# A 3x3 convolution on one core: input pairs loaded two at a time, two output pairs stored by one transfer each, and one image's store cut in halves

## The chip, the core and the metric

The kernel runs on one core of a Trainium2 chip. The metric is the device time of one execution in microseconds (us). Before the change it is 127.98 us, the median of three runs (127.71 to 128.12). One further execution was profiled; that profile is what is read here.

The engines that appear: PE multiplies matrices, DVE and POOL do elementwise work, ACT copies and converts, SP and ACT issue DMA transfers. A transfer is split over 16 DMA engines. What SP issues runs on queue q1 of each of them, what ACT issues on queue q10, so each DMA engine has one queue from SP and one from ACT.

## The reference

```python
batch, c_in, h, w, c_out = 16, 64, 64, 64, 128      # float32
x_pad = np.pad(x, ((0, 0), (0, 0), (1, 1), (1, 1)), mode='constant')
for b, co, ci, kh, kw:
    output[b, co] += weight[co, ci, kh, kw] * x_pad[b, ci, kh:kh+h, kw:kw+w]
```

The input is 16 images of 64 channels (16.8 MB), the output 16 images of 128 channels (33.6 MB). All of it passes through the DMA engines once.

## The kernel before

**Tiling.** Two images of 64 channels fill the 128 partitions, so the batch is eight pairs, p = 0 to 7 in the code. A pair's input is one tile `raw` of 128 partitions with 16 KB each, 2 MB in all. Its output is two tiles `ot` (one for each image, 128 output channels, 16 KB in each partition), again 2 MB each. Output rows are made two at a time, with a transform over the rows (Winograd's): for each block of 8 row pairs PE makes three groups of sums in PSUM, U (line 180), A (190) and Bt (193). ACT copies U to `ut` (184), and DVE adds `ut` to A for the even rows (192) and to Bt for the odd rows (195) and writes `ot`. A pair has four such blocks.

**Getting a pair ready.** Before PE can start on a pair, POOL must have made the row sums `ss` (line 70; for pair p+1 it is called at the start of pair p), and ACT must have converted the rows to 16 bits, `xs` (line 103; a quarter in each block of the pair before, right behind the block's two copies of U). ACT works in program order: a conversion that waits for its input holds up the copies of U behind it.

**Where things lie.** There are ten places of 16 KB in each partition, `home0` to `home9`, shared by inputs and outputs. `raw_home` and `out_home` (44, 45) say which place a pair's input and its two images take. A place is written anew only when its former content has been used or stored: a wait on a conversion, a sum, or the landing of a transfer.

**Transfers.** SP issues the weights, then the inputs of pairs 0 to 5 at the start (52 to 54). After block 3 of each pair SP stores the pair's first image (197), and after the first two pairs it loads pair 6 and pair 7 (200, 201). The second image goes onto a list (199) and is stored by ACT in the next pair, behind the copies of U (186, 187; for pair 0 not before block 2 of pair 1). The last pair's two images are stored in halves, after block 1 and after block 3 (`halves`, 123, 124). SP, too, works in order: a load that waits for its place holds up the stores behind it. So the order of work around the change is the order written in the program, engine by engine.

Of the kernel before, what the change touches and what calls it, by code (L numbers as in the profile page):

```python
# [8 lines left out]
F32 = mybir.dt.float32  # L9
# [4 lines left out]
def kernel(  # L14
# [6 lines left out]
    nc = tc.nc  # L21
    B, CI, H, W = x.shape
    CO = weight.shape[0]
    assert H == 64 and W == 64 and CI == 64 and CO == 128 and B % 2 == 0
    NP = B // 2
    RB = 8

    keep = tc.keep_in_program_order
    x_rows = x.rearrange("b c h w -> (b c) h w")
    out_rows = out.rearrange("b co h w -> b co h w")  # L30
# [5 lines left out]
    opool = ctx.enter_context(tc.tile_pool(name="opool", bufs=1))  # L36
# [4 lines left out]
    nc.sync.dma_start(w_raw, w_flat)  # L41


    raw_home = [0, 1, 2, 3, 4, 5, 0, 6]
    out_home = [(6, 7), (8, 9), (1, 2), (7, 3), (8, 4), (9, 5), (1, 2), (7, 3)]
    raws = {}

    def load(p):
        raws[p] = opool.tile([128, H, W], F32, tag=f"home{raw_home[p]}", name="raw")
        keep(nc.sync.dma_start(raws[p], x_rows[128 * p : 128 * p + 128, :, :]))  # L50

    AHEAD = 6
    for p in range(AHEAD):
        load(p)
    x0 = raws[0]
    ident = const.tile([128, 128], F16)
    make_identity(nc, ident)
# [7 lines left out]
    def sums(eng, p, src, lo, n):  # L65
        if p not in ss:
            ss[p] = spool.tile([128, H // 2, W], F16, tag="ss", name="ss")
        v = src.rearrange("p (j i) c -> p j i c", i=2)
        keep(
            eng.tensor_add(  # L70
                ss[p][:, lo : lo + n, :], v[:, lo : lo + n, 0, :], v[:, lo : lo + n, 1, :]
            )
        )
# [26 lines left out]
    def cast(copy, p, lo, hi):  # L100
        if p not in xs:
            xs[p] = xpool.tile([128, H, W], F16, tag="xs", name="xs")
        keep(copy(xs[p][:, lo:hi, :], raws[p][:, lo:hi, :]))  # L103
# [17 lines left out]

    whole = {3: (0, 64)}
    halves = {1: (0, 32), 3: (32, 64)}
    cuts_of = [(whole, whole)] * (NP - 1) + [(halves, halves)]

    def store(eng, p, b2, ot, lo, hi):
        return eng.dma_start(
            out_rows[2 * p + b2, :, lo:hi, :],
            ot.rearrange("p j i c -> p (j i) c")[:, lo:hi, :],
        )  # L130

    for p in range(NP):
        if p + 1 < NP:
            for lo in (0, 16):
                sums(nc.gpsimd, p + 1, raws[p + 1], lo, 16)
        ots = [
            opool.tile([128, H // 2, 2, W], F32, tag=f"home{k}", name="ot")
            for k in out_home[p]
        ]
        for blk in range(4):  # L140
            j0 = blk * RB

            def group(wi_rows):

                tiles = [
                    psum.tile([128, RB, W], F32, tag="acc", name="acc") for _ in range(2)
                ]
                n = 3 * len(wi_rows)
                i = 0
                for wi, off in wi_rows:  # L150
                    for kw in (1, 0, 2):
                        c_lo, c_hi = max(0, 1 - kw), min(W, W + 1 - kw)
                        for b2 in range(2):
                            p0 = 64 * b2
                            lo, hi = j0, j0 + RB
                            if off is None:
                                rhs = ss[p][p0 : p0 + 64, lo:hi, c_lo + kw - 1 : c_hi + kw - 1]
                            else:
                                while 2 * lo + off < 0:
                                    lo += 1  # L160
                                while 2 * (hi - 1) + off > H - 1:
                                    hi -= 1
                                first = 2 * lo + off
                                last = 2 * (hi - 1) + off
                                rhs = xs[p][
                                    p0 : p0 + 64,
                                    first : last + 1 : 2,
                                    c_lo + kw - 1 : c_hi + kw - 1,
                                ]
                            nc.tensor.matmul(  # L170
                                tiles[b2][:, lo - j0 : hi - j0, c_lo:c_hi],
                                Wt[p0 : p0 + 64, wi, kw, :],
                                rhs,
                                start=i == 0,
                                stop=i == n - 1,
                            )
                        i += 1
                return tiles

            U = group([(G1, None)])  # L180
            us = []
            for b2 in range(2):
                ut = upool.tile([128, RB, W], F32, tag="ut", name="ut")
                keep(nc.scalar.copy(ut, U[b2]))  # L184
                us.append(ut)
            while held and (p, blk) not in ((1, 0), (1, 1)):
                keep(store(nc.scalar, *held.pop(0)))
            for piece in later.get((p, blk), ()):
                cast(nc.scalar.copy, *piece)
            A = group([(G21, 1), (G0, -1)])  # L190
            for b2 in range(2):
                nc.vector.tensor_add(ots[b2][:, j0 : j0 + RB, 0, :], A[b2], us[b2])  # L192
            Bt = group([(G01, 0), (G2, 2)])
            for b2 in range(2):
                nc.vector.tensor_add(ots[b2][:, j0 : j0 + RB, 1, :], Bt[b2], us[b2])  # L195
            if blk in cuts_of[p][0]:
                keep(store(nc.sync, p, 0, ots[0], *cuts_of[p][0][blk]))
            if blk in cuts_of[p][1]:
                held.append((p, 1, ots[1], *cuts_of[p][1][blk]))
            if blk == 3 and p + AHEAD < NP:  # L200
                load(p + AHEAD)
    while held:
        keep(store(nc.scalar, *held.pop(0)))

# [29 lines left out]
```

## Time and profile before

| what | value |
|---|---|
| median of three runs | 127.98 us |
| the profiled execution, device time | 128.16 us |
| its span, from the first to the last event shown | 126.4 us |
| PE busy | 107.9 us, 85% of the span |
| DVE busy | 84.2 us, 67% |
| ACT busy | 65.8 us, 52% |
| POOL busy | 37.2 us, 29% |
| bytes moved by DMA | 50.77 MB, mean 402 GB/s |
| transfers on q1 / q10 | 18 / 9 |
| clock that PE was granted | 0.963 in the mean; full speed until the last matmul |

How to read it: a busy share is a mean over the whole span. The bytes moved, divided by the span, are a rate; whether it is near what the DMA engines can do is seen from how busy they are in each stretch of the span, and from how long one packet takes.

### The profile page before, as it was taken

The numbers are of one execution on the slowest core, as the hardware profiler recorded it, in microseconds if no ns is written. First come the engines' busy times: TensorE is split into PE (matmuls) and PEld (weight loads), VectorE is DVE, ScalarE is ACT, GpSimd is POOL, SyncE is SP. The second block draws the span as 40 slices with busy tenths as digits, with TensorE's granted clock in tenths as the row PEclk, the third lists the DMA queues.
The fourth block names the chain that finished last, engine by engine and source line by source line (L and its number), as shares of the span: only waits on it lengthen the run. The fifth ranks groups of instructions, "written<-read, shape, count | busy, mean of one in ns | idle before, by whom it ended". The sixth has DMA issues, their size and how long they took to land.

```text
span 126.4 us, 2450 instructions
## 1 busy us (share of the span) xinstructions
PE 107.9 (85%) x984; PEld 53.1 (42%) x984; DVE 84.2 (67%) x135; ACT 65.8 (52%) x98; POOL 37.2 (29%) x23
## 2 busy tenths in 40 slices
PE   0689999999999999999999999999999999970000
PEld 0534444444444444444444555555555555530000
DVE  1029987877777778777729977777877787771000
ACT  4128569966666657666664666666666633320000
POOL 2227685900590049004900193009400000000000
PEclk9999999999999999999999999999999999999555
DMA  5899999999899999999999999999999999999960
GB/s 161 363 441 446 425 420 420 430 451 394 332 430 430 438 425 420 428 430 441 425 410 430 425 446 430 415 425 425 436 441 415 425 410 420 449 392 420 438 254 10
DMA packets 3898, 50.77 MB, mean 402 GB/s; under 512 B 432, under 2 KB 432, under 8 KB 560
## 3 DMA queue, kind: packets, MB, share of 16 engines
q1 hardware_dynamic: 2592, 33.85, 64.1%
q10 hardware_dynamic: 1296, 16.78, 31.2%
q8 instruction: 7, 0.11, 0.3%
q14 instruction: 3, 0.02, 0.0%
HBM read 17.07 MB, written 33.55 MB: 401 GB/s over the span
## 4 chain that ended last, share of the span: by engine, by line
PE 79%; DMA 6%; DVE 2%; issue 1%; DVEq 0%; ACT 0%; SPq 0%; ACTq 0%
PE acc L170 79%; DMA raw<-in_x_dram 6%; DVE ot L192 1%; DVE ss L70 1%; DVE ot L195 0%; DVEq L229 0%; ACT ut L184 0%; SPq L41 0%; DVEq L192 0%; ACTq L184 0%
## 5 line engine op out<-in xcount | busy, mean ns | idle before, releaser
L170 PE MATMUL acc<-xs,Wt 64*128 64x504 f16 (+3 forms) x768 | 90.3, 373 | 0.2 <-DVE ot L192 0.2
L170 PEld LDWEIGHTS <-Wt 64*128 64x128 f16 x960 | 50.4, 94 | 53.9 <-issue 1.9
L192 DVE TENSOR_TENSOR ot<-acc,ut 128x512 f32<-128x512 f32 x64 | 41.1, 684 | 21.6 <-PE acc L170 16.2
L184 ACT COPY ut<-acc 128x512 f32<-128x512 f32 x64 | 34.4, 589 | 38.1 <-issue 21.5
L70 POOL TENSOR_TENSOR ss<-raw 128x1024 f16<-128x1024 f32 x14 | 32.8, 2364 | 45.1 <-issue 33.2
L195 DVE TENSOR_TENSOR ot<-acc,ut 128x512 f32<-128x512 f32 x64 | 41.0, 683 | 0.0
L103 ACT CAST xs<-raw 128x1024 f16<-128x1024 f32 (+1 forms) x30 | 31.6, 1060 | 3.4 <-DMA raw<-in_x_dram 3.3
L170 PE MATMUL acc<-ss,Wt 64*128 64x504 f16 (+1 forms) x192 | 28.7, 377 | 0.6 <-DVE ss L70 0.6
L70 DVE TENSOR_TENSOR ss<-raw 128x512 f16<-128x512 f32 x4 | 3.3, 866 | 7.5 <-DMA raw<-in_x_dram 7.5
L88 PE MATMUL wp<-ident,w 128*64 128x128 f16 x18 | 1.3, 328 | 4.3 <-POOL w L59 4.3
L103 POOL CAST xs<-raw 128x1024 f16<-128x1024 f32 (+1 forms) x2 | 3.0, 1518 | 4.6 <-DMA raw<-in_x_dram 4.6
L94 PE MATMUL warm<-blank 128*128 128x400 f32 x6 | 3.4, 726 | 0.0
L88 PEld LDWEIGHTS <-w 128*64 128x64 f16 x18 | 1.1, 209 | 4.3 <-POOL w L59 4.3
L94 PEld LDWEIGHTS warm<-blank 128*128 128x128 f32 x6 | 1.6, 292 | 1.3 <-issue 1.0
L95 ACT CAST Wt<-wp 128x384 f16<-128x384 f32 x1 | 0.5, 479 | 3.0 <-PE wp L88 3.0
L95 ACT ACT_TABLE_LOAD x1 | 1.3, 1283 | 0.7 <-PEq L218 0.7
L59 POOL CAST w<-w_raw 128x576 f16<-128x576 f32 x1 | 0.7, 663 | 2.3 <-DMA w_raw<-in_weight_dram 2.3
L91 DVE MEMSET blank<- 128x400 f32 x1 | 0.4, 392 | 0.9 <-PEq L218 0.9
L108 ACT CAST Wt<-wp 128x384 f16<-128x384 f32 x1 | 0.5, 479 | 0.5 <-DVE Wt L98 0.5
L97 DVE TENSOR_TENSOR Wt<-wp,Wt 128x384 f16<-128x384 f32 x1 | 0.6, 550 | 0.0
L98 DVE TENSOR_TENSOR Wt<-wp,Wt 128x384 f16<-128x384 f32 x1 | 0.5, 548 | 0.0
L109 ACT CAST Wt<-wp 128x384 f16<-128x384 f32 x1 | 0.5, 485 | 0.0
(6 smaller groups left out, 0.9 us busy)
## 6 DMA issues: line engine op xcount, KB each, us to landing
raw<-in_x_dram SPq DMA_DIRECT2D x8, 2048.0 KB, 24.3
out_dram<-ot SPq DMA_DIRECT2D x7, 2048.0 KB, 23.0
out_dram<-ot ACTq DMA_DIRECT2D x7, 2048.0 KB, 15.1
out_dram<-ot SPq DMA_DIRECT2D x2, 1024.0 KB, 12.3
out_dram<-ot ACTq DMA_DIRECT2D x2, 1024.0 KB, 11.9
w_raw<-in_weight_dram SPq DMA_DIRECT2D x1, 288.0 KB, 2.8
```

Source lines behind the costliest of these rows:

```text
L59: keep(nc.gpsimd.tensor_copy(w16, w_raw))
L70: eng.tensor_add(ss[p][:, lo : lo + n, :], v[:, lo : lo + n, 0, :], v[:, lo : lo + n, 1, :])
L88: nc.tensor.matmul(wp[q : q + 64, k * CO : k * CO + CO], w16[:, t::9], ident)
L94: nc.tensor.matmul(warm[:, 0:400], blank[:, 0:128], blank)
L95: keep(nc.scalar.copy(wrow(G1), wps[1]))
L97: keep(nc.vector.tensor_sub(wrow(G21), wps[2], wrow(G1)))
L98: keep(nc.vector.tensor_sub(wrow(G01), wps[0], wrow(G1)))
L103: keep(copy(xs[p][:, lo:hi, :], raws[p][:, lo:hi, :]))
L170: nc.tensor.matmul(tiles[b2][:, lo - j0 : hi - j0, c_lo:c_hi], Wt[p0 : p0 + 64, wi, kw, :], rhs, start=i == 0, stop=i == n - 1,)
L184: keep(nc.scalar.copy(ut, U[b2]))
L192: nc.vector.tensor_add(ots[b2][:, j0 : j0 + RB, 0, :], A[b2], us[b2])
L195: nc.vector.tensor_add(ots[b2][:, j0 : j0 + RB, 1, :], Bt[b2], us[b2])
```

## The change

1. The ten places of 16 KB become six of 16 KB (`a` to `f`) and two of 32 KB (`g`, `h`).
2. Pairs 2 and 3 are loaded by one transfer of 4 MB into `g`, pairs 4 and 5 by one of 4 MB into `h`. In each partition, the row of one pair is followed by that of the next; in memory the two rows are 2 MB apart. Pairs 0 and 1 are loaded as before.
3. The images of pair 3 (in `g`) and of pair 5 (in `h`) are each stored by one transfer of 4 MB from SP after block 3. Before, SP stored the first image and ACT the second. Pair 7's images lie in `g`, and are stored in four halves as before.
4. Pair 6 is loaded by SP after pair 1 (before: after pair 0), into `c`, which held pair 0's first image. Pair 7 is loaded after pair 2 (before: after pair 1), into `f`, which held pair 1's second image.
5. The first image of pair 6 is stored in halves, after block 1 and after block 3.
6. The places of the outputs change accordingly (`out_home`).

In all there are 24 transfers in place of 27: 17 from SP (18 before) and 7 from ACT (9 before). What PE, DVE, ACT and POOL compute, and the order in which they do so, is the same.

```diff
-    raw_home = [0, 1, 2, 3, 4, 5, 0, 6]
-    out_home = [(6, 7), (8, 9), (1, 2), (7, 3), (8, 4), (9, 5), (1, 2), (7, 3)]
+    out_home = ["cd", "ef", "ab", "g", "de", "h", "ab", "g"]
     raws = {}

-    def load(p):
-        raws[p] = opool.tile([128, H, W], F32, tag=f"home{raw_home[p]}", name="raw")
-        keep(nc.sync.dma_start(raws[p], x_rows[128 * p : 128 * p + 128, :, :]))
-
-    AHEAD = 6
-    for p in range(AHEAD):
-        load(p)
+    def load(ps, home):
+        raw = opool.tile([128, len(ps), H, W], F32, tag=home, name="raw")
+        src = x_rows[128 * ps[0] : 128 * ps[0] + 128 * len(ps), :, :]
+        keep(nc.sync.dma_start(raw, src.rearrange("(k p) h w -> p k h w", p=128)))
+        for k, p in enumerate(ps):
+            raws[p] = raw[:, k, :, :]
+
+    def homes(p):
+        if len(out_home[p]) == 2:
+            return [
+                opool.tile([128, H // 2, 2, W], F32, tag=h, name="ot") for h in out_home[p]
+            ]
+        both = opool.tile([128, 2, H // 2, 2, W], F32, tag=out_home[p], name="both")
+        both_of[p] = both
+        return [both[:, 0, :, :, :], both[:, 1, :, :, :]]
+
+    both_of = {}
+
+    load([0], "a")
+    load([1], "b")
+    load([2, 3], "g")
+    load([4, 5], "h")
...
-    cuts_of = [(whole, whole)] * (NP - 1) + [(halves, halves)]
+    cuts_of = [(whole, whole)] * (NP - 2) + [(halves, whole), (halves, halves)]
+    together = (3, 5)
+    load_behind = {1: ([6], "c"), 2: ([7], "f")}
...
-        ots = [
-            opool.tile([128, H // 2, 2, W], F32, tag=f"home{k}", name="ot")
-            for k in out_home[p]
-        ]
+        ots = homes(p)
...
+            if p in together:
+                if blk == 3:
+                    keep(
+                        nc.sync.dma_start(
+                            out_rows[2 * p : 2 * p + 2].rearrange("b c h w -> c b h w"),
+                            both_of[p].rearrange("p b j i c -> p b (j i) c"),
+                        )
+                    )
+                continue
...
-            if blk == 3 and p + AHEAD < NP:
-                load(p + AHEAD)
+            if blk == 3 and p in load_behind:
+                load(*load_behind[p])
```

## The prediction, made before the changed kernel ran

> **What bounds the kernel now.** I read the page's rows by slices and its DMA queues first.
>
> ```profile
> PEclk9999999999999999999999999999999999999555
> DMA  5899999999899999999999999999999999999960
> GB/s 161 363 441 446 425 420 420 430 451 394 332 430 430 438 425 420 428 430 441 425 410 430 425 446 430 415 425 425 436 441 415 425 410 420 449 392 420 438 254 10
> ...
> q1 hardware_dynamic: 2592, 33.85, 64.1%
> q10 hardware_dynamic: 1296, 16.78, 31.2%
> q8 instruction: 7, 0.11, 0.3%
> ```
>
> A slice is 3.16 us. The DMA engines are full from the second slice to the 38th, at 410 to 450 GB/s whatever is loaded or stored. The two queues take 64.1 + 31.2 = 95.3% of 16 engines' span: 120.4 us of work for each engine, in a span of 126.4. Then windows of the end:
>
> ```profile
> 100.00:104.00 4.00, 4.00 (x42) 2.14 (x38) 3.40 (x7) 1.15 (x3) 0.00 (x0) 1.00 1.01 414
> 104.00:114.00 10.00, 9.03 (x85) 4.55 (x79) 7.82 (x13) 3.15 (x6) 0.00 (x0) 1.00 0.99 422
> 114.00:121.00 7.00, 0.00 (x0) 0.00 (x0) 0.21 (x1) 0.00 (x0) 0.00 (x0) 0.72 1.02 430
> 121.00:122.00 1.00, 0.00 (x0) 0.00 (x0) 0.00 (x0) 0.00 (x0) 0.00 (x0) 0.50 0.59 246
> 122.00:123.00 1.00, 0.00 (x0) 0.00 (x0) 0.00 (x0) 0.00 (x0) 0.00 (x0) 0.50 0.29 123
> 123.00:124.00 1.00, 0.00 (x0) 0.00 (x0) 0.00 (x0) 0.00 (x0) 0.00 (x0) 0.50 0.08 33
> 124.00:125.00 1.00, 0.00 (x0) 0.00 (x0) 0.00 (x0) 0.00 (x0) 0.00 (x0) 0.50 0.04 16
> ```
>
> The last two columns are the DMA engines' busy share and GB/s. DVE is done at 114.2; the DMA engines work off what is queued at full rate to 121, then they finish one by one: a share of 0.06 is one engine, so from 123 on it is about one. In the trace's packet records that last engine's final packet ends at 124.7, the one before it at 123.4, the first at 121.3. A 16 KB packet takes 0.611 us and the next starts 0.607 after it; chained by these times, an engine has no gap over 0.5 us, and the gaps that there are (0.3 to 0.5 us at 101.7, where pair 6's stores had just been issued) are on engines that finish early. So the bound is the work of the slowest DMA engine, which never waits.
>
> Why one is slower: besides its 16th of the data, an engine serves "instruction" packets of 16 KB (q8). At 19.2 us one takes 0.94 us and stretches the data packet behind it from 0.61 to 1.10, 1.4 us in all; the next load's last share lands 1.3 us behind the other fifteen. The sixth load's last share is 2.1 us behind the second-last, after another such packet at 31.4. Two on one engine is the likely reason for the late end; the other engines end in a range that none or one explains.
>
> Then the waits and the chain of waits, for PE's side:
>
> ```profile
> DVE ot L192 <- DMA out_dram<-ot: 2.9, 1, 2.9
> ...
> 9.54 55.41 PE acc L170 x516
> 64.95 0.00 ACTq L184
> 64.95 0.04 issue
> 64.99 0.57 ACT ut L184
> 65.57 0.45 issue
> 66.02 0.69 DVE ot L192
> 66.71 0.04 issue
> 66.75 44.88 PE acc L170 x406
> ```
>
> PE is continuous but for one break: at pair 4 DVE waits 2.95 us (to 65.4) for home 8, where pair 1's first image, issued at 36.3, needed 29.0 us to land behind pair 6's load. Pairs start on DVE every 12.8 us; from pair 3 (50.24) to pair 5 (76.39) it is 26.15, so the stall costs 26.15 - 25.6 = 0.55 us in the end.
>
> **The change, part by part.** Profiled time before 128.16, of which 126.4 is span and 1.8 lies around it; it is 0.2 above the median, 127.98, and I forecast against the median.
>
> *Merged loads.* Loads 0, 1, 2 land at 8.8, 13.7, 18.5: 4.87 us apart, 8 packets of 0.607 = 4.86. A boundary between transfers costs 0.01 us, so two fewer give nothing. Four issues of some 0.45 us instead of six all lie ahead of 4 us. What they move is the landing: pair 2 is usable when pair 3 is. Load 3 lands 22.1 us behind its issue at 2.6, that is at 24.7. POOL's sums for pair 2 (at 20.27 now) move to 24.7 and end at 29.4; PE uses them at 35.4: hidden, 6 us to spare. ACT's first conversion of pair 2 stands at 24.36: it waits 0.4 us, takes 1.06, ends at 25.8, and the next copy of U comes at 26.56. Hidden by 0.8 us; beyond that each us late would hold ACT's copies, then PE. Pair 4 lands with pair 5 at 36.7; POOL wants it at 45.9. Cost 0.
>
> *Packets of merged transfers.* An engine has 4 x 16 = 64 packets in the four merged transfers, alternating between rows 2 MB apart. No transfer of the trace does this. Below: 0, since pair 0's two images, on q1 and q10, alternate rows 2 MB apart, and their packets (37 to 42 us) have a mean of 0.613 against 0.611 for loads alone; that packets get faster is excluded, as none between 50 and 120 us is shorter than 0.605. Above: q1's slowest stretch after 40 us (100 to 105) has a mean of 0.632: 64 x 0.021 = 1.3 us. I take 0, by the nearer row.
>
> *Order on q1.* With S0 for the store of the first image of pair 0 and L6 for the load of pair 6, the queue holds, behind the loads of the start, S0 L6 S1 L7 S2 S3 before and S0 S1 L6 S2 L7 S3 after. The landings before are 46.4, 56.2, 65.3, 74.4, 80.5, 89.7; the queue's places stay, so I read S1 at 56.2, L6 65.3, S2 74.4, L7 80.5 or earlier (ACT's queue has no image of pair 3 any more). Needs: DVE at pair 4 wants S1 at 62.5: the stall goes, 0.55 us of compute. POOL wants L6 at 72.2 and L7 at 85.0; DVE wants S2's place at 88.6 and all of pair 3's stored by 101.4. Cost 0. On SP, L6 now waits for S0 (46.4), and S2's store behind it is due at 49.1; L7 waits for pair 1's second image (36.9 + 18.6 = 55.5), and pair 3's store is due at 61.9. No delay.
>
> *Pairs 3 and 5 on SP alone.* ACT loses two issues of 0.34 us beside idle time. One queue feeds an engine as well as two: the loads ran on q1 alone, and from 76 to 80, with q10 nearly empty, the busy share is 1.00. Cost 0.
>
> *Pair 6 in halves.* 1 MB is ready at 94.9 - 0.55 = 94.4 instead of 100.8. It fills the gap at 101.7, 0.3 to 0.5 us on the early engines, 0 on the last. One more boundary: 0.01.
>
> *Sum.* Compute ends 0.55 earlier, at 113.6, in front of 10 us of queued transfers: hidden. DMA: three transfers fewer, -0.02. Last engine: 0. 127.98 - 0.02 = 127.96; I say **127.9**. The 0.55 us would cost or gain time only without that cover: compute would have to slip by over 3 us before the last engine ran dry.
>
> **Rivals.**
>
> 1. *The recovered compute reaches the end* (faster). If the last engine, too, runs short near 101.7, earlier data helps it by the compute gain: 127.98 - 0.55 = 127.4. For: some engines did run dry. Against: none of those was the last one. 15%.
> 2. *Instruction packets fall on other engines* (faster or slower). Their order follows PE's program, which is unchanged, and the three times lie within 0.41 us: against. If the last engine loses one, the next one, 1.3 us earlier, sets the end: 126.7, 10%. If a third falls on one engine: 127.98 + 1.4 = 129.4, 7%.
> 3. *Merged packets run slower* (slower). Place: each DMA engine's queue q1, at the 64 packets of the four merged transfers. Price up to 1.3 us: 129.3. It decides from 0.38 / 64 = 6 ns a packet on. For: such alternation on one queue isn't in the trace. Against: on two queues it is, at 2 ns. 18%. The Trainium skill ("DMA: Bandwidth & Descriptors", Latency and other measured facts) knows such a slowdown, to 164 GB/s where the rows of neighbouring partitions lie 2 MB apart; 16.8 MB at that rate instead of 429 GB/s would add some 63 us, an estimate from that page. Here partitions lie 16 KB apart, as before, and no run shows the other layout.
> 4. *A boundary between transfers costs an engine time* (faster). Between loads it is 0.01 us; between stores on a late engine no gap is over 0.5, so three fewer give at most 1.5: 126.5. Against: the landings 4.87 us apart. 2%. The Trainium skill (same page, Rules for kernel authors) advises to merge many small transfers, and its Anatomy of one DMA gives a transfer issued from GpSimd a fixed cost of about 2.0 us; by that, 3 fewer would give 6 us. This trace shows no such cost on a busy engine.
>
> **How the numbers follow.** Forecast 48%. A measurement here tells about 0.3% (0.38 us) from no change. Within it: the forecast, 0.48. Faster: 0.15 + 0.10 + 0.02 = 0.27. Slower: 0.18 + 0.07 = 0.25. The range goes down to rival 2's 126.7 and up to 129.0, which holds rival 3 up to 16 ns a packet; outside are the top of rival 3, the third packet, and what lies under 126.7: some 17 in 100. The forecast's own range is 127.6 to 128.3.
>
> **What would show it.** Right: in the windows of the end one engine still ends 1 to 2 us behind the next, at about 124 to 125; the 2.9 us wait of L192's line on a store is gone; PE's chain has no break near 65; DVE ends near 113.6; no window of 4 us with a DMA share under 0.95 between 4 and 120 us but for the dip near 31. Wrong, if DMA shares sag while pairs 2 to 5 load, or at 62 to 90; if ACT or POOL waits on a load for over 1 us beyond the first; or if the DMA engines end together.

## The result, and the profile after

The changed kernel takes 127.84 us (median of 21 runs, 127.65 to 128.27), the kernel before, run beside it, 128.19 us (21 runs, 127.71 to 128.56). The ratio is 0.9977, with a 95% interval of 0.9969 to 0.9985: by the ratio 0.29 us less (0.19 to 0.40), a small gain that these 21 runs tell from nothing, and less than the 0.3% that the prediction set as the bound of no change. Some executions come out longer as a whole, and runs more than 1.5% above the fastest of their kernel are left out of every range and ratio below. The profiled execution took 127.71 us, its span is 125.9.

The page's rows by slices and its DMA queues, of the changed kernel:

```profile
DMA  5999999999899999999999999999999999999960
GB/s 166 365 442 427 432 422 432 437 432 411 323 432 437 424 422 422 440 437 427 416 427 422 442 422 427 427 427 427 432 427 432 437 396 442 437 398 432 427 284 18
...
q1 hardware_dynamic: 2960, 38.04, 72.2%
q10 hardware_dynamic: 1008, 12.58, 23.5%
q8 instruction: 7, 0.11, 0.3%
```

Queue q1 has taken over the second images of pairs 3 and 5 from q10, 4.2 MB; the two together hold 95.7% of the span, as much work as before. The DMA engines are as full as they were, and serve as many instruction packets. Then windows, with the DMA engines' busy share and GB/s in the last two columns:

```profile
60.00:80.00 20.00, 20.00 (x192) 9.18 (x188) 15.74 (x26) 13.03 (x19) 8.29 (x4) 1.00 1.01 428
...
114.00:121.00 7.00, 0.00 (x0) 0.00 (x0) 0.00 (x0) 0.00 (x0) 0.00 (x0) 0.55 1.01 425
121.00:122.00 1.00, 0.00 (x0) 0.00 (x0) 0.00 (x0) 0.00 (x0) 0.00 (x0) 0.50 0.60 254
122.00:123.00 1.00, 0.00 (x0) 0.00 (x0) 0.00 (x0) 0.00 (x0) 0.00 (x0) 0.50 0.24 98
123.00:124.00 1.00, 0.00 (x0) 0.00 (x0) 0.00 (x0) 0.00 (x0) 0.00 (x0) 0.50 0.10 41
124.00:125.00 1.00, 0.00 (x0) 0.00 (x0) 0.00 (x0) 0.00 (x0) 0.00 (x0) 0.50 0.02 8
```

The end has the form that it had: full rate to 121, then the engines finish one by one. In the packet records the last engine's final packet ends at 124.59 (124.69 before), the next engine's at 123.52. Now compute: two pieces of the chain of waits (start, length, what), and two groups of the waits (total, times, longest):

```profile
9.70 101.61 PE acc L184 x948
...
113.25 0.60 DVE both L209
```

```profile
POOL ss L85 <- DMA raw<-in_x_dram: 8.3, 2, 6.5
...
ACT xs L118 <- DMA raw<-in_x_dram: 3.7, 2, 3.4
```

PE runs from 9.70 to 111.31 without the break at 65; DVE waits for no store any more and ends at 113.85 instead of 114.2. (The first load landed 0.15 us later in this execution, which takes back a part.) POOL waits 6.5 us for pair 2, which now arrives with pair 3; nobody waits for POOL behind that. Of ACT's 3.7 us, 3.4 are its first conversion's at the start, and 0.3 are the merged load's.

The two profiled executions differ by 0.45 us. The parts: final packet 0.10, from there to the landing of the last transfer 0.18 (0.63 against 0.45), from the landing to the span's end 0.17 (1.06 against 0.89). No one of these is large, and a single execution is no better than the spread of the runs; so the source of the gain had to be looked for in other kernels.

### The profile page after: what moved, and what is told of

Its sections match the earlier page's. It is cut to its first block, busy times and chain, and to the rows that moved or that the text cites. A ratio compares the mean times of both kernels' runs of the same rounds, so it can differ in the third digit from the quotient of the medians.

```text
span 125.9 us, 2440 instructions
## 1 busy us (share of the span) xinstructions
PE 107.9 (86%) x984; PEld 49.8 (40%) x984; DVE 84.5 (67%) x135; ACT 65.8 (52%) x98; POOL 37.1 (30%) x23
## 2 busy tenths in 40 slices
DMA packets 3978, 50.77 MB, mean 403 GB/s; under 512 B 384, under 2 KB 384, under 8 KB 512
## 4 chain that ended last, share of the span: by engine, by line
PE 81%; DMA 6%; DVE 2%; issue 1%; DVEq 0%; SPq 0%
PE acc L184 81%; DMA raw<-in_x_dram 6%; DVE both L206 1%; DVE ss L85 1%; DVE both L209 0%; DVEq L252 0%; SPq L41 0%; DVEq L206 0%
## 5 line engine op out<-in xcount | busy, mean ns | idle before, releaser
L184 PE MATMUL acc<-xs,Wt 64*128 64x504 f16 (+3 forms) x768 | 87.1, 373 | 0.0
L184 PEld LDWEIGHTS <-Wt 64*128 64x128 f16 x960 | 46.8, 94 | 56.4 <-issue 0.7
L206 DVE TENSOR_TENSOR ot<-acc,ut 128x512 f32<-128x512 f32 x40 | 25.7, 685 | 12.4 <-PE acc L184 11.3
L184 PE MATMUL acc<-ss,Wt 64*128 64x504 f16 (+1 forms) x192 | 26.0, 377 | 0.2 <-DVE ss L85 0.2
L209 DVE TENSOR_TENSOR ot<-acc,ut 128x512 f32<-128x512 f32 x40 | 25.7, 682 | 0.0
L206 DVE TENSOR_TENSOR both<-acc,ut 128x512 f32<-128x512 f32 x24 | 15.5, 685 | 8.4 <-PE acc L184 7.8
L209 DVE TENSOR_TENSOR both<-acc,ut 128x512 f32<-128x512 f32 x24 | 15.4, 683 | 0.0
L109 PE MATMUL warm<-blank 128*128 128x400 f32 x6 | 3.9, 815 | 0.0
L110 ACT CAST Wt<-wp 128x384 f16<-128x384 f32 x1 | 0.5, 479 | 3.0 <-PE wp L103 3.0
L123 ACT CAST Wt<-wp 128x384 f16<-128x384 f32 x1 | 0.5, 480 | 0.5 <-DVE Wt L113 0.5
L112 DVE TENSOR_TENSOR Wt<-wp,Wt 128x384 f16<-128x384 f32 x1 | 0.6, 550 | 0.0
```

The lines of the kernel that those rows point to most:

```text
L109: nc.tensor.matmul(warm[:, 0:400], blank[:, 0:128], blank)
L110: keep(nc.scalar.copy(wrow(G1), wps[1]))
L112: keep(nc.vector.tensor_sub(wrow(G21), wps[2], wrow(G1)))
L123: keep(nc.scalar.copy(wrow(G0), wps[0]))
L184: nc.tensor.matmul(tiles[b2][:, lo - j0 : hi - j0, c_lo:c_hi], Wt[p0 : p0 + 64, wi, kw, :], rhs, start=i == 0, stop=i == n - 1,)
```

## The experiments

Diffs are against the changed kernel, where nothing else is said. Ratios are to the kernel before, run on the same chip, with 95% intervals; a profile is of one execution.

### Is compute hidden, and what makes one DMA engine late?

Two tests of the bound. The first delays compute at pair 4, by about the stall that the change had removed and more:

```diff
             A = group([(G21, 1), (G0, -1)])
+            if (p, blk) == (4, 0):
+                for _ in range(4):
+                    keep(nc.vector.tensor_add(w_raw[:, 0:512], w_raw[:, 0:512], w_raw[:, 0:512]))
             for b2 in range(2):
```

> The changed kernel with four additions of 128x512 on a dead tile on DVE ahead of pair 4's first addition: DVE is 2.6 us later there, PE some 1.5 to 2 us (a stall like the one before the change). Prediction's theory: hidden by the last engine's 10 us of queued work; DVE ends near 115.5 to 116, the time is that of the changed kernel, ratio 0.998. Rival C (compute reaches the end): +0.5 to +2.0, ratio 1.002 to 1.013.

Measured: 127.82 us (127.69 to 128.13, 11 runs), ratio 0.9978 [0.9969, 0.9988], as the changed kernel's. The chain of waits of this kernel:

```profile
68.06 44.88 PE acc L184 x406
...
114.91 0.60 DVEq L255
```

PE's chain is broken at pair 4 again, resumes at 68.06, later than it did before the change (66.75), and DVE ends near 115.5. The final packet still ends at 124.57. So the recovered stall is hidden in full, and the gain is not compute's.

The second takes PE's program away, and with it the instruction packets:

```diff
-                n = 3 * len(wi_rows)
+                n = len(wi_rows)
...
-                    for kw in (1, 0, 2):
+                    for kw in (1,):
...
-            A = group([(G21, 1), (G0, -1)])
+            A = Bt = U
...
-            Bt = group([(G01, 0), (G2, 2)])
```

> The changed kernel without most of the matmuls: of each block only the middle tap of U is made, and DVE adds it to ut for both rows; the sums A and Bt are left out. All transfers, ACT, DVE and POOL work stay. PE has under 256 instructions left. Theory (the last DMA engine is late because it serves two instruction packets): no instruction packet of 16 KB on q8; the landings of load 3 and load 5 spread by 0.6 us instead of 1.9 and 3.5; the engines end within 0.7 us, at about 121.5, the span is about 123.0, the time 124.8. Rival (that engine is slow by itself, or through the packets' order): the last engine ends 2 to 3 us behind the mean as now, span 125.9, time 127.8. If the compute were the bound, the span would fall by over 10 us, as DVE's work of 84 us is all that is left.

Measured: 125.04 and 126.27 us in two runs, ratio 0.9808 [0.9767, 0.9849]. The faster of them was profiled. Its queues and its windows of the end:

```profile
q1 hardware_dynamic: 2960, 38.04, 73.6%
q10 hardware_dynamic: 1008, 12.58, 23.9%
q14 instruction: 2, 0.02, 0.0%
```

```profile
114.00:121.00 7.00, 0.00 (x0) 0.00 (x0) 0.00 (x0) 0.00 (x0) 0.00 (x0) 0.50 1.00 421
121.00:122.00 1.00, 0.00 (x0) 0.00 (x0) 0.00 (x0) 0.00 (x0) 0.00 (x0) 0.50 0.20 82
122.00:123.00 1.00, 0.00 (x0) 0.00 (x0) 0.00 (x0) 0.00 (x0) 0.00 (x0) 0.50 0.00 0
```

Same bytes, same data packets, no row q8, and the DMA engines end together: the share is 1.00 to 121 and 0.00 from 122. The last transfer's sixteen landings lie within 1.3 us (5.3 in the changed kernel). The span is 123.3, 2.6 us shorter (124.5 in the other run, 1.4 shorter). An engine that is slow by itself is thereby ruled out, and the instruction packets are the likely cause of the late end. They are not quite shown to be it: with less work on PE the last stores are also issued some 16 us earlier (98.0 against 113.9), which was not tried by itself. That two such packets meet on one engine is not shown. One expectation failed: the landings of the two merged loads spread by 0.7 and 1.8 us (2.0 and 3.5 in the changed kernel), not by 0.6 both.

A probe was to tell which engine it is: the first images of pairs 0 and 1 stored in groups of partitions, which spread over fewer DMA engines.

```diff
-            if blk in cuts_of[p][0]:
+            if blk in cuts_of[p][0] and p < 2:
+                lo = 0
+                for n in ((64, 14, 12, 10, 8, 20), (64, 52, 6, 4, 2))[p]:
+                    keep(
+                        nc.sync.dma_start(
+                            out_rows[2 * p, lo : lo + n, :, :],
+                            ots[0].rearrange("p j i c -> p (j i) c")[lo : lo + n, :, :],
+                        )
+                    )
+                    lo += n
+            elif blk in cuts_of[p][0]:
```

> The changed kernel with the first images of pairs 0 and 1 stored in groups of partitions (64, 14, 12, 10, 8, 20 and 64, 52, 6, 4, 2) by one transfer each. It asks which of the 16 DMA engines is the late one. The Trainium skill (DMA: Bandwidth & Descriptors, Why a DMA increments its semaphore by 16 and not by 1) says that such a transfer runs on the lowest-numbered 16, 14, 12, 10, 8, 10 and 16, 13, 6, 4, 2 engines. If the late engine is among those of a transfer, the last of its landings stands some 1.8 us or more behind the others; if not, it doesn't. So the landings narrow the engine down to two. If none of the transfers, the full ones included, has a lone late landing, the lateness isn't that of one engine.

Measured: 138.0 us in one run. Of pair 0's groups, the last landing stands 1.7, 2.1 and 2.6 us behind the one before it in those of 64, 14 and 12 partitions (on 16, 14 and 12 engines, by the landings counted), but also 1.4 us in that of 10 and 1.9 us in that of 8, and 0.4 us in that of 20, which uses 10 engines. So the landings do not single out an engine. The groups themselves also disturbed the run: the page's row of rates falls to between 272 and 351 GB/s in the slices from 37 to 68 us, at full busy shares.

```profile
GB/s 159 409 433 433 428 419 438 433 428 322 390 313 279 272 313 315 289 351 342 337 241 428 414 433 433 423 438 414 438 438 419 428 426 421 423 421 428 428 281 31
```

So the probe is inconclusive, and relieving a late engine by such groups was not tried: they cost some 10 us here, and the next engine ends only 1 us earlier.

### Is it the way the program ends?

In the trace SP waits at the end for the transfers' semaphores in five instructions some 62 ns apart, in a fixed order, and the transfers take eight semaphores in turn. So the number of transfers decides how many waits still lie behind the last landing's. Before, its semaphore was in the first of the five waits, after the change in the fourth: 1.06 against 0.89 us from landing to end. Three kernels change that number, the first by adding three transfers to the changed kernel:

```diff
-                keep(store(nc.sync, p, 0, ots[0], *cuts_of[p][0][blk]))
+                cut = cuts_of[p][0][blk]
+                for lo, hi in ((0, 32), (32, 64)) if p in (1, 2, 4) else (cut,):
+                    keep(store(nc.sync, p, 0, ots[0], lo, hi))
```

> The changed kernel with the first image of pairs 1, 2 and 4 stored by two transfers of 1 MB, both issued after block 3: 27 transfers as before the change, the same bytes in the same order. Theory E (order of the waits at the end): behind the last landing SP still has five waits to go through, in a fixed order of the DMA semaphores, some 0.06 us each; with 24 transfers the last landing is on the semaphore that is waited for in the fourth instruction, with 27 in the first. So the last landing stands 1.05 us before the span's end again (after: 0.89), the time is 0.19 above the changed kernel's, ratio to before about 0.999. Rival P (each transfer costs DMA time): 0.1 for each of three, +0.3, ratio 1.000. Rival C (the gain is that of the compute, whose stall is gone): no change against the changed kernel, ratio 0.998.

Measured: ratio 1.0026 [1.0002, 1.0049], 127.82 to 129.59 us in 10 runs. From landing to end it is 0.99 us in the profile, more than half of the shift that was expected, but the time is higher than that accounts for, and spread over 1.8 us. The second adds five transfers to the kernel before, by cutting stores of pairs 2 to 5 in halves (here the diff is against the kernel before):

```diff
-                keep(store(nc.sync, p, 0, ots[0], *cuts_of[p][0][blk]))
+                cut = cuts_of[p][0][blk]
+                for lo, hi in ((0, 32), (32, 64)) if p in (2, 3, 4, 5) else (cut,):
+                    keep(store(nc.sync, p, 0, ots[0], lo, hi))
...
-                held.append((p, 1, ots[1], *cuts_of[p][1][blk]))
+                cut = cuts_of[p][1][blk]
+                for lo, hi in ((0, 32), (32, 64)) if p in (2,) else (cut,):
+                    held.append((p, 1, ots[1], lo, hi))
```

> The kernel before with the first image of pairs 2 to 5 and the second image of pair 2 stored by two transfers of 1 MB each: 32 transfers, so that the last two are on the same semaphores as in the changed kernel. Theory E: the last landing is 0.89 before the span's end instead of 1.05, 0.19 faster than before, ratio 0.9985. Rival P: five transfers more cost 0.5, ratio 1.004. Rival C: the stall at pair 4 is still there, ratio 1.000.

Measured: ratio 1.0062 [1.0026, 1.0099], 127.95 to 129.64 us in 10 runs. It tests something else than it was made for. With eight semaphores in turn, a transfer is not issued until the one eight places before it has landed; with more and smaller transfers that comes sooner. Two pieces of its chain of waits, and one of its windows:

```profile
24.09 31.63 DMA raw<-in_x_dram
...
55.80 0.34 ACTq L127
```

```profile
100.00:104.00 4.00, 4.00 (x42) 2.13 (x40) 3.04 (x5) 2.85 (x5) 0.00 (x0) 1.00 0.56 231
```

Pair 6's load is issued at 24.09 as before the change (24.00) and lands at 55.73. Eight places behind it stands the added transfer for pair 2's second image, which ACT cannot issue until then. It goes out at 55.80, and what stands behind it in ACT's program waits with it: the next conversion starts at 56.18, behind 6.0 us of idle time, though its own input had long landed. Compute ends at 116.6, and the DMA engines run half empty from 100 to 104, at a share of 0.56. So the third adds four transfers of 32 bytes to the kernel before, ahead of all stores:

```diff
+    tiny = const.tile([1, 4, 8], F32)
+    for n in range(4):
+        keep(nc.sync.dma_start(tiny[:, n, :], x_rows[n : n + 1, 0, 0:8]))
```

> The kernel before with four more transfers of 32 bytes, on one DMA engine, behind the six loads of the start: 31 transfers, the last two on the semaphores that are waited for third and fourth at the end. Theory E (order of the waits at the end): some 0.06 to 0.17 us less between the last landing and the span's end than before (1.05), ratio 0.9985 to 0.9995. Rival P (each transfer costs DMA time): four more, +0.4, ratio 1.003. Rival C (the compute's stall is what is gained): stall still there, 1.000.

Measured: 128.26 us (127.93 to 128.82), ratio 1.0009 [0.9995, 1.0022]. The profile has the 0.89 us from landing to end, and the time doesn't show them. Nor do other kernels follow it: from landing to end it is 0.83 us at a ratio of 0.9987 (stores merged alone, below), 0.93 at 0.9977 (loads apart) and 0.93 at 1.0021 (stores apart). The order of the waits at the end is real in the trace, but the gain is not explained by it: that theory fell.

### Which part of the change brings it?

One part undone at a time. Pair 6's first image whole:

```diff
-    cuts_of = [(whole, whole)] * (NP - 2) + [(halves, whole), (halves, halves)]
+    cuts_of = [(whole, whole)] * (NP - 2) + [(whole, whole), (halves, halves)]
```

> The changed kernel with the first image of pair 6 stored by one transfer after block 3, as before the change: 23 transfers. Prediction's theory: the halves fill a gap that only early DMA engines have, so the time is that of the changed kernel to within 0.1, ratio 0.997 to 0.999. Rival (the halves bring the gain): the gain goes, ratio 1.000, and the last engine shows a gap near 101.

Four loads of 2 MB in place of the two of 4 MB, into the same places:

```diff
-        src = x_rows[128 * ps[0] : 128 * ps[0] + 128 * len(ps), :, :]
-        keep(nc.sync.dma_start(raw, src.rearrange("(k p) h w -> p k h w", p=128)))
         for k, p in enumerate(ps):
             raws[p] = raw[:, k, :, :]
+            keep(nc.sync.dma_start(raws[p], x_rows[128 * p : 128 * p + 128, :, :]))
```

> The changed kernel with pairs 2 to 5 loaded by four transfers of 2 MB in place of two of 4 MB, into the same places: 26 transfers. Prediction's theory: a boundary between loads costs 0.01, and alternating rows cost nothing, so the time is that of the changed kernel to within 0.1 to 0.2 (the waits at the end fall into another order), ratio 0.997 to 0.999. Rival (merging the loads brings the gain): ratio 1.000. Rival 3 of the prediction (alternating rows are slower): faster than the changed kernel, ratio under 0.997.

The new places and order alone: loads apart as above, pair 6 whole as above, and the images of pairs 3 and 5 stored apart, the second by ACT in the next pair:

```diff
-    together = (3, 5)
+    together = ()
```

> The changed kernel with its places and its order of loads, but with nothing merged and nothing halved anew: pairs 2 to 5 loaded one by one, both images of pairs 3 and 5 stored apart (the second by ACT), pair 6's first image whole; 27 transfers, the end's waits as before. If the gain is that of the order and the places (late loads of pairs 6 and 7, no stall): ratio 0.998. If it is that of the merged stores, or of the halves, or of the order of the end's waits: 1.000.

The same, but with the images of pairs 3 and 5 stored by one transfer each from SP, so that the edits are those of the first two diffs of this part:

> As the kernel before this one, but with the images of pairs 3 and 5 stored by one transfer each from SP; 25 transfers, SP's last store on the semaphore that is waited for last. If the merged stores bring the gain: ratio 0.998, and this differs from the order alone. If the order and the places do: 0.998 for both. If the halves do: 1.000 for both.

The changed kernel with nothing but `together = ()`:

> The changed kernel with the images of pairs 3 and 5 stored apart, the second by ACT; loads merged and pair 6 in halves as in the change; 26 transfers. If the merged stores bring the gain: ratio 1.000. If not: 0.998. The prediction's theory says that the DMA engines are full either way, so no difference over 0.1 us from the changed kernel.

This left two things in one: a merged store is one transfer in place of two, and it runs on SP's queue alone. The last kernel parts them, with two transfers of 2 MB each, both from SP:

```diff
-                    keep(
-                        nc.sync.dma_start(
-                            out_rows[2 * p : 2 * p + 2].rearrange("b c h w -> c b h w"),
-                            both_of[p].rearrange("p b j i c -> p b (j i) c"),
-                        )
-                    )
+                    for b2 in range(2):
+                        keep(store(nc.sync, p, b2, ots[b2], *whole[3]))
```

> The changed kernel, but each of pairs 3 and 5 stored by two transfers of 2 MB, both from SP, one behind the other, in place of one of 4 MB; 26 transfers, as in the kernel whose second images of these pairs went by ACT (ratio 1.0021). If it is the queue that counts (all of a pair's output on q1, so that q10 is empty and each DMA engine works off one queue), the ratio is that of the changed kernel, 0.997 to 0.999, pair 7's load lands at 75 us, not at 84, and the packets of 60 to 80 us move at 428 GB/s. If it is the merging itself (one transfer of 4 MB in place of two), the ratio is that of the stores apart, 1.001 to 1.004, and the windows of 60 to 80 us show about 424 GB/s. By the prediction's cost of nothing for both it would be 0.999 to 1.000.

Measured (11 or 12 runs each but for the first):

| kernel | second images of pairs 3 and 5 | loads 2 to 5 | pair 6 | transfers | range, us | ratio |
|---|---|---|---|---|---|---|
| changed kernel | SP, merged | merged | halves | 24 | 127.65 to 128.27 | 0.9977 [0.9969, 0.9985] |
| pair 6 whole | SP, merged | merged | whole | 23 | 127.70 to 128.27 | 0.9985 [0.9974, 0.9995] |
| stores merged alone | SP, merged | apart | whole | 25 | 127.76 to 128.36 | 0.9987 [0.9976, 0.9998] |
| loads apart | SP, merged | apart | halves | 26 | 127.65 to 128.14 | 0.9977 [0.9967, 0.9987] |
| two stores from SP | SP, apart | merged | halves | 26 | 127.80 to 128.12 | 0.9986 [0.9975, 0.9997] |
| stores apart | ACT | merged | halves | 26 | 127.84 to 129.12 | 1.0021 [0.9997, 1.0044] |
| order alone | ACT | apart | whole | 27 | 127.94 to 129.49 | 1.0045 [1.0024, 1.0067] |

The column that parts these seven is the queue. With both images from SP the ratio is 0.9977 to 0.9987, whatever the loads and pair 6, with 23 to 26 transfers; with the second from ACT it is 1.0021 and 1.0045, and the runs scatter over 1.3 and 1.6 us in place of 0.3 to 0.6. For the order alone 0.998 or 1.000 was expected; 1.0045 is neither. Two transfers from SP do as well as one, within 0.1%: it isn't the merging. The two kernels with 26 transfers and merged loads that differ in the queue alone have intervals that just touch, at 0.9997. Pair 6's halves are worth 0.1% at most, and the intervals with and without overlap.

Two kernels limit this reading. The one with three more transfers has both images of pairs 3 and 5 from SP, and is as slow and scattered (1.0026, over 1.8 us): cutting other stores in halves does it too. And the kernel before stores second images by ACT without such a scatter (0.62 us in 29 runs, on the chip of the two kernels with ACT's stores). So ACT's stores are seen to cost only in the new order of loads and places.

Where the time goes with the ACT queue is not compute. The chain of waits of the kernel with the stores apart has PE's unbroken piece, no longer than that of the changed kernel, and so has that of the order alone in an execution of 128.72 us:

```profile
9.65 101.61 PE acc L184 x948
```

Its load of pair 7 lands at 84.1 (75.1 in the changed kernel and with two stores from SP), still ahead of the 85.0 at which POOL wants it. Windows, first with the stores apart, then the order alone, then two stores from SP, and one of the stores merged alone:

```profile
60.00:80.00 20.00, 20.00 (x190) 9.18 (x188) 15.78 (x26) 13.07 (x19) 8.24 (x4) 1.00 1.00 424
...
124.00:125.00 1.00, 0.00 (x0) 0.00 (x0) 0.00 (x0) 0.00 (x0) 0.00 (x0) 0.50 0.10 41
```

```profile
60.00:80.00 20.00, 20.00 (x192) 9.18 (x188) 15.73 (x26) 13.11 (x19) 8.28 (x4) 1.00 1.01 424
...
124.00:125.00 1.00, 0.00 (x0) 0.00 (x0) 0.00 (x0) 0.00 (x0) 0.00 (x0) 0.50 0.12 49
```

```profile
60.00:80.00 20.00, 20.00 (x192) 9.18 (x190) 15.63 (x26) 13.05 (x20) 8.40 (x4) 1.00 1.00 426
...
124.00:125.00 1.00, 0.00 (x0) 0.00 (x0) 0.00 (x0) 0.00 (x0) 0.00 (x0) 0.50 0.04 16
```

```profile
124.00:125.00 1.00, 0.00 (x0) 0.00 (x0) 0.00 (x0) 0.00 (x0) 0.00 (x0) 0.50 0.08 33
```

With ACT's stores the engines are as busy and move 424 GB/s from 60 to 80 where the changed kernel moves 428: 20 x 4 / 428 = 0.19 us of work. Two stores from SP, expected at 428, show 426, and the kernel before, with ACT's stores, 425. From 124 to 125 between one and two engines are still at work with ACT's stores (0.10 and 0.12; one is 0.06), and the final packets end at 125.2 and 125.6. But the stores merged alone, all from SP, show 0.08 and a final packet at 125.3 in their slowest execution (128.36 us, the one profiled), so the end of a single execution does not tell the queues apart. The packet records say more: the time of the 16 KB packets that start after 40 us, beyond 0.607 us each, summed and divided by 16 engines, is 0.85 to 0.90 us in the six profiles in which pairs 3 and 5 go by SP and the other transfers are those of the change (the delayed pair 4 among them), and 0.94, 1.04, 1.13 and 1.17 in the four in which ACT stores the second image (stores apart, the kernel before, that with four tiny transfers, the order alone). But these are single executions, the kernel with three more transfers has 0.69 and is slower (its profiled execution was its fastest, 127.82), and why a packet is longer when both queues hold stores is not seen in any record. That the queue of these stores makes the difference in the new order is shown; how it does it stays open, and so does what slows the kernel with three more transfers. The old order with all of pairs 3 and 5 from SP was not tried.

No version that does the whole work beat the changed kernel.

## Why the prediction was right

The forecast was 127.9, and no change that can be told; 127.84 came, with the ratio within 0.3%. That the two times agree to 0.1 us is in part luck: the kernel before, run beside it, took 128.19, not the 127.98 that the sum starts from, and 127.96 was rounded down. Point by point:

- **The bound.** Compute can be made later by more than the stall without a trace in the time (0.9978), so that part is confirmed. That the late end comes from instruction packets is supported (span 123.3 and 124.5 without them, 123.0 expected); two of them on one engine stays a guess. Rival 1 falls: the 0.55 us stayed hidden. Rival 2 did not happen: again one engine ends 1.07 us behind the next. Of the signs, no window of 4 us between 4 and 120 has a share under 0.97 but that from 32 to 36 (0.93). One sign of being wrong did come, POOL's wait of 6.5 us on a load, where over 1 us was named; the working itself had moved these sums to 24.7, so the sign was drawn too wide. And "410 to 450 GB/s" from the second slice on leaves out slices at 363, 394, 332 and 392 in the row that is shown.
- **Merged loads, and the packets in them.** Nothing, as forecast: merged or apart, 0.9977 both. Pairs 3 and 5 were usable at 24.84 and 36.83 (24.7 and 36.7 forecast), and the two waits were those named, POOL's hidden, ACT's 0.3 us (0.4). Rivals 3 and 4 fall with it: no price per merged packet, and no gain per transfer saved, since with pairs 3 and 5 from SP the ratios do not follow the number of transfers from 23 to 26. The Trainium skill ("DMA: Bandwidth & Descriptors", Rules for kernel authors) says to have 1 MiB or more in a DMA for bandwidth; all of these loads have, and the runs show no gain beyond 2 MB.
- **Order on q1.** Read by places in the queue, the landings came out: S1 at 56.28 (56.2 forecast), L6 at 65.40 (65.3); S2 at 70.26 and L7 at 75.08, earlier than the 74.4 and 80.5 read, since ACT's queue was emptier (with the stores apart they are at 74.7 and 84.1). The 2.9 us wait is gone, and DVE ends at 113.85 (113.6).
- **Where a size was off.** The sum had -0.02 us; -0.29 (-0.40 to -0.19) was measured. The term at fault is "Pairs 3 and 5 on SP alone", put at 0 because "one queue feeds an engine as well as two". In the new order one queue does better than two: the two kernels that differ in this term alone, both with loads apart, stand at 0.9987 and 1.0045 of 128.14 us, 0.74 us apart. Nor is the cost of the order 0 by itself: with ACT's stores kept it is 0.45% (0.24 to 0.67), some 0.58 us slower, with PE's chain unbroken; why is not known. The two terms have opposite signs, and nearly cancel. That is why the sum came out so well, and it is luck: the prediction foresaw neither. The row that the step rested on, a busy share of 1.00 with one queue nearly empty, could not tell it: the share is 1.00 either way, and only the rate beside it (424 against 426 to 428) differs. The Trainium skill (same page and section) says that spreading transfers over several issuing engines doesn't help bandwidth, as they run on the same 16 DMA engines; the runs agree, and go further: in the new order the spreading costs.

## What to carry to other kernels

When DMA engines are full from start to end, look at how the last of them ends: here neither compute time that was regained nor loads that were merged beyond 2 MB changed the time. A busy share of 1.00 does not say that the work is done at the best rate; read the rate and the packets' length beside it, and try the same transfers on one queue and on two. A result near nothing may be two effects of opposite sign: undo the parts one by one before calling each of them nothing.

## What the runs showed of the hardware

- **Instruction packets and the end of a kernel bound by transfers.** With seven packets of 16 KB (0.11 MB of 50.77) the DMA engines end over 3 us apart; in the kernel without them, which also has little work for PE, they end some 1 us apart and the span is 1.4 to 2.6 us shorter.
- **Semaphores of transfers, eight in turn.** They tie the number of transfers to the order of waiting at the end (0.89 or 1.06 us behind the last landing) and make a transfer wait for the one eight before it; cutting stores smaller held ACT for 6.0 us at a store, and the conversion behind it, in a kernel with no other change.
- **Transfers of few partitions.** Stores of groups of 2 to 64 partitions with 16 KB each, among full ones, brought the rate down to between 272 and 351 GB/s for 30 us, with the DMA engines shown as fully busy (one run).
